# Residual x added by a transfer that adds on writing, in a streaming-encoder block

## The chip, the core and the metric

The kernel runs on one core of one Trainium2 chip. A core has TensorE for matrix products (PE in the profile; its weight loads, which run beside the products, are PEld), VectorE (DVE), ScalarE (ACT), GpSimd (POOL) and SyncE (SP), each with an instruction queue of its own that is worked off in order. Transfers between the chip's memory and the core's on-chip memory are issued from a queue (SP, ACT or POOL) and carried out by 16 DMA engines. The metric is the device time of one execution in microseconds (us).

## What is computed

One layer on x of 256 rows and 4096 columns, all in float32. After a norm, `xn @ w_in` gives the inputs of two branches, chunked attention and a convolution module, which yield y_a and y_c (2048 columns each). What matters here comes next:

```python
h = h + jnp.concatenate([y_a, y_c], axis=-1) @ w_out[i]      # residual: h is x here
gate = jax.nn.sigmoid(rms_norm(h, ple_norm_g[i]) @ w_ple_gate[i] + b_ple_gate[i])
h = h + gate * (p[i] @ w_ple[i])
return rms_norm(h, final_g)
```

So the output product (4096 by 4096) gets x added, the sum's rows need their sum of squares for the next norm, and the sum is the operand of the gate product (4096 by 4096).

## The kernel before

The 256 rows are two halves of 128 (index h), and columns go in blocks of 512. A product with a 4096-row weight is made by `mixed_product` for two column blocks (index j) at a time. It walks over 16 pairs of 128-row weight blocks in an order written out by hand (`dense`, `late`, `final`, ...). Every float32 operand is split in a high and a low part: `parts_of` lets ScalarE cast the weight block to the high part (wh, line 204) and VectorE subtract it to get the low part (wl, line 205), and TensorE makes three products of them. The pairs marked `*` are not made plainly (24 matmuls) but in seven combined products (21 matmuls), for which VectorE also adds weight blocks (ua, ub, lines 426 to 431). These seven go to four accumulators of the result, acc[h][j], and four helper accumulators P1, P5, P6 and P7. When the last seven-product pair is done, `on_helpers` combines the helpers into what has to be added to or subtracted from each quarter. In `helper_sums` (lines 464 to 471) that is one ScalarE copy and four VectorE additions.

Weight blocks come by transfers from SP's queue into five buffers, high and low parts have three buffers each. The order of instructions on each engine is the program's, except that a planner (of the tile framework) with a cost model of its own may bring instructions forward as their inputs and buffers allow. `later` is a queue of small pieces of work, and `fill` takes some from it after each pair.

The stage around the change is the loop over c0 = 0, 2, 4, 6 at lines 1045 to 1071: four output products, each for two column blocks. Before each, SP's queue loads the two blocks of x into the tiles `hc` (line 1049). `on_helpers` (lines 1054 to 1061) adds P1 to the first quarter of hc in place, builds the helpers' sums in scratch tiles z, and adds or subtracts those to the other three quarters. After the product, line 1070 adds the four accumulators to hc, and line 1071 queues four square sums (`square_sum`, line 500, ScalarE) for the norm. After the loop all that is left in `later` is done and `rstd_of` makes r_h, with a power on GpSimd.

Then come four gate products (`gated_pair` and a last one written out). Their operand is made from the tiles hc by `h_ahead`: TensorE transposes, ScalarE and VectorE split (lines 156 and 157) and combine them (lines 257 to 273). r_h is used first in the gate product's own `on_helpers` (line 1091).

Of the kernel before, what the change touches and what calls it, by code (L numbers as in the profile page):

```python
# [10 lines left out]
F32 = mybir.dt.float32  # L11
F32R = mybir.dt.float32r
AF = mybir.ActivationFunctionType
ALU = mybir.AluOpType
AX = mybir.AxisListType

P = 128
NB = 512
# [7 lines left out]
def hybrid_block(  # L26
# [23 lines left out]
    nc = tc.nc  # L50
    _, T, D = x.shape
    NH = T // P
# [15 lines left out]
    def pool(name, bufs, stack=ctx, side=0, **kw):  # L68
        return stack.enter_context(tc.tile_pool(name=name, bufs=bufs, side=sides[side], **kw))

    cpool = pool("cpool", 1)
    act = pool("act", 8)
# [107 lines left out]
    later = deque()  # L180

    def fill(n):
        for _ in range(min(n, len(later))):
            later.popleft()()
# [141 lines left out]

    def mixed_product(
        w, col, lhs, comb, order, on_helpers, ahead=None, fills=(0,), on_begin=None, apart=NB,
        left=(), begin=None,
    ):  # L330
# [64 lines left out]
        for n, (pair, seven) in enumerate(order):  # L395
# [59 lines left out]
            if n == last_seven:  # L455
                on_helpers(helper)
# [4 lines left out]
    tt, stt = nc.vector.tensor_tensor, nc.vector.scalar_tensor_tensor  # L461
    QUARTERS = ((0, 0), (1, 0), (0, 1), (1, 1))

    def helper_sums(helper, z):


        nc.scalar.copy(z[1][0], helper["P1"])
        tt(z[1][0], helper["P6"], z[1][0], ALU.add)
        tt(z[0][1], helper["P5"], z[1][0], ALU.add)
        tt(z[1][0], helper["P7"], z[1][0], ALU.add)  # L470
        tt(z[1][1], helper["P5"], z[1][0], ALU.add)

    def sum_tiles():

        t = [spool.tile([P, NH, NB], F32, tag="stage", name="z") for _ in range(2)]
        return t, [[t[j][:, h] for j in range(2)] for h in range(NH)]

    def scaled_pair(w, col, apart, order, r, fills, **kw):

        t, z = [], []  # L480

        def on_helpers(helper):
            for dst, src in zip((t, z), sum_tiles()):
                dst.extend(src)
            nc.scalar.activation(z[0][0], helper["P1"], AF.Identity, scale=r[:, :1])
            helper_sums(helper, z)
            for h, j in QUARTERS[1:]:
                nc.scalar.activation(z[h][j], z[h][j], AF.Identity, scale=r[:, h : h + 1])

        c = mixed_product(w, col, xT, xS, order, on_helpers, fills=fills, apart=apart, **kw)  # L490
        for h, j in QUARTERS:
            stt(
                z[h][j], c[h][j], r[:, h : h + 1], z[h][j],
                ALU.mult, ALU.subtract if j else ALU.add,
            )
        return t
# [443 lines left out]
    for c0, order in zip(range(0, CW // NB, 2), point):  # L940
        row = broadcast_row(b_pw, c0 * NB, 2 * NB, tag="stage")
        rows = [row[:, j * NB : (j + 1) * NB] for j in range(2)]
        ys, z = [], []
# [4 lines left out]
        def on_helpers(helper):  # L948
            y_tiles()
            z.extend([ys[j][:, h, :] for j in range(2)] for h in range(NH))  # L950
            tt(z[0][0], helper["P1"], rows[0], ALU.add)
            helper_sums(helper, z)
            for h, j in QUARTERS[1:]:
                tt(z[h][j], z[h][j], rows[j], ALU.subtract if j else ALU.add)

        acc = mixed_product(w_pw[0], c0 * NB, uS, uC, order, on_helpers)
# [35 lines left out]
    def before_last(make):  # L992

        return lambda pair: make(0) if pair == dense[-1][0] else None
# [29 lines left out]
    hs, hT, hS = [], [], []  # L1024
# [17 lines left out]
                embedding()  # L1042

    ssq_h = cpool.tile([P, NH, D // NB], F32, name="ssq_h")
    for c0 in range(0, D // NB, 2):
        for j in range(2):
            hc = act.tile([P, NH, NB], F32, tag="act", name="hc")
            c = c0 + j
            nc.sync.dma_start(
                hc, x[0, :, c * NB : (c + 1) * NB].rearrange("(h q) n -> q h n", q=P)  # L1050
            )
            hs.append(hc)

        def on_helpers(helper):
            _, z = sum_tiles()
            h00, h01, h10, h11 = (hs[c0 + j][:, h, :] for h in range(NH) for j in range(2))
            tt(h00, helper["P1"], h00, ALU.add)
            helper_sums(helper, z)
            tt(h01, h01, z[0][1], ALU.subtract)
            tt(h10, h10, z[1][0], ALU.add)  # L1060
            tt(h11, h11, z[1][1], ALU.subtract)

        acc = mixed_product(
            w_out[0], c0 * NB, yT, yS, dense if c0 else late, on_helpers,
            ahead=y_ahead if c0 == 0 else before_last(h_ahead) if c0 + 2 == D // NB else None,
            fills=(2,),
        )
        for h, j in QUARTERS:
            hc = hs[c0 + j][:, h, :]
            tt(hc, acc[h][j], hc, ALU.add)  # L1070
            later.append(partial(square_sum, ssq_h[:, h, c0 + j : c0 + j + 1], hc))
    fill(len(later))
    r_h = rstd_of(ssq_h, D, "r_h")

# [49 lines left out]
    c0 = n_f - 2  # L1124
    _, z = sum_tiles()
# [17 lines left out]
    def on_helpers(helper):  # L1143
# [4 lines left out]
    acc, add_left = mixed_product(  # L1148
        w_ple_gate[0], c0 * NB, hT, hS, final, on_helpers, fills=(4,), on_begin=on_begin,
        left=[None] * 3 + [kept] * 3,  # L1150
    )
# [119 lines left out]
```

## Time and profile before

| | us |
|---|---|
| three runs, median | 2039.71 |
| three runs, lowest and highest | 2039.58, 2039.95 |
| span of the profiled execution | 2038.9 |
| TensorE busy in it | 2021.0 |
| VectorE busy | 1905.7 |
| ScalarE busy | 1184.3 |
| GpSimd busy | 8.1 |

For the profiled execution the span from its first to its last instruction is what the profile gives; it lies 0.8 us under the median of the runs. A row of instructions in the profile reads: line, engine, operation, what it writes <- what it reads, how many, then durations and times. A row of a timeline reads: start in us, length in us, the instruction, and in brackets how long its engine stood idle before it and what ended that. In a row of waits, "A <- B: 0.2, 1, 0.2" means that A waited for B 0.2 us in total, once, the longest 0.2. "DMA to landing" is the time from a transfer's issue until its data is there. In a table of windows each row has the stretch, its length, and each engine's busy time with its instruction count, the granted clock of TensorE, the busy share of the DMA engines and what they moved.

### The profile page before, as it was taken

The page shows a single profiled execution, that of the slowest core. Times are in us where ns is not written, and L with a number is a line of the kernel's source. Part 1 is how long each engine was busy: PE and PEld are TensorE (multiplying, and loading weights), DVE is VectorE, ACT ScalarE, POOL GpSimd, SP SyncE. Part 2 cuts the span into 40 slices and gives each one's busy share as a digit, 9 for nine tenths or more (in the row PEclk, how much of TensorE's full clock was granted, in tenths as well). Part 3 has the DMA queues.
Part 4 walks back from the last instruction along what each step waited for, and adds up shares of the span by engine and source line. Part 5 has one row for each costly group of instructions (what it writes and reads, how often), then busy time and mean ns, then how long its engine had stood idle before and what let it go on. Part 6 is the DMA issues. An engine that isn't in the chain of part 4 may idle for free.

```text
span 2038.9 us, 26038 instructions
## 1 busy us (share of the span) xinstructions
PE 2021.0 (99%) x9106; PEld 1661.3 (81%) x9106; DVE 1905.7 (93%) x2720; ACT 1184.3 (58%) x1527; POOL 8.1 (0%) x19
## 2 busy tenths in 40 slices
PE   9999999999999999999999999999999999999997
PEld 7888888887888888888888888888888888888876
DVE  7999999899989998878899999999999999999998
ACT  7655535554555545576555656676565666655555
POOL 0000000000000000000000000000000000000000
PEclk9999999999999999999999999999999999999999
DMA  8566665666656665556666666676666656666765
GB/s 294 188 198 204 200 191 167 203 191 186 184 178 211 202 184 186 178 192 197 187 216 206 197 214 201 215 243 204 211 205 205 206 190 208 198 222 205 234 206 180
DMA packets 161853, 412.29 MB, mean 202 GB/s; under 512 B 12974, under 2 KB 16190, under 8 KB 161722
## 3 DMA queue, kind: packets, MB, share of 16 engines
q1 hardware_dynamic: 161072, 409.80, 62.9%
q8 instruction: 71, 1.16, 0.2%
q10 hardware_dynamic: 650, 0.84, 0.1%
q14 instruction: 60, 0.49, 0.1%
HBM read 406.39 MB, written 4.19 MB: 201 GB/s over the span
## 4 chain that ended last, share of the span: by engine, by line
PE 86%; DVE 10%; issue 2%; ACT 1%; DMA 0%; POOLq 0%; POOL 0%; ACTq 0%; DVEq 0%
PE acc L370 60%; PE acc_P L370 15%; PE acc L218 8%; DVE wl L205 4%; DVE cv L677 3%; PE tmp_ps L170 1%; DVE ul L205 1%; ACT wh L204 0%; PE tmp_ps L834 0%; PE tmp_ps L849 0%; DVE ub L431 0%; PE tmp_ps L867 0%; DVE ub L430 0%; DVE ua L426 0%; DVE ua L427 0%
## 5 line engine op out<-in xcount | busy, mean ns | idle before, releaser
L370 PE MATMUL acc<-wh,big_t 128*128 128x512 f32 x3788 | 1173.6, 391 | 0.9 <-DVE y_c L964 0.7
L204 ACT CAST wh<-wt 128x1024 fp32r<-128x1024 f32 (+1 forms) x737 | 714.7, 980 | 558.4 <-PE acc L370 335.4
L205 DVE TENSOR_TENSOR wl<-wt,wh 128x1024 fp32r<-128x1024 f32 (+1 forms) x737 | 823.7, 1130 | 48.2 <-ACT wh L204 43.0
L370 PEld LDWEIGHTS acc<-wh,big_t 128*128 128x128 f32 x3788 | 708.2, 188 | 147.9 <-DVE y_c L964 1.1
L370 PE MATMUL acc<-wl,big_t 128*128 128x512 f32 x1894 | 730.7, 391 | 0.2 <-DVE wl L205 0.2
L370 PEld LDWEIGHTS acc<-wl,big_t 128*128 128x128 f32 x1894 | 355.2, 188 | 75.7 <-DVE wl L205 2.0
L677 DVE SCALAR_TENSOR_TENSOR cv<-uT,dw,cv 128x255 f32<-128x255 f32 (+20 forms) x480 | 205.1, 463 | 1.3
L204 ACT CAST uh<-ub 128x1024 fp32r<-128x1024 f32 x122 | 128.3, 1052 | 123.9 <-DVE ub L431 99.9
L218 PE MATMUL acc<-wh,big_t 128*128 128x512 f32 x560 | 173.9, 392 | 0.0
L204 ACT CAST uh<-ua 128x1024 fp32r<-128x1024 f32 x122 | 128.6, 1054 | 72.5 <-DVE ua L427 65.3
L205 DVE TENSOR_TENSOR ul<-ub,uh 128x1024 fp32r<-128x1024 f32 x122 | 148.8, 1219 | 7.7 <-ACT uh L204 6.9
L370 PE MATMUL acc_P<-uh,big_t 128*128 128x512 f32 x504 | 154.4, 392 | 0.1
L205 DVE TENSOR_TENSOR ul<-ua,uh 128x1024 fp32r<-128x1024 f32 x122 | 148.6, 1218 | 0.6 <-ACT uh L204 0.4
L218 PEld LDWEIGHTS acc<-wh,big_t 128*128 128x128 f32 x560 | 105.5, 189 | 21.6
L370 PEld LDWEIGHTS acc_P<-uh,big_t 128*128 128x128 f32 x504 | 93.5, 188 | 22.3 <-ACT uh L204 3.6
L218 PE MATMUL acc<-wl,big_t 128*128 128x512 f32 x280 | 109.6, 392 | 0.0
L426 DVE TENSOR_TENSOR ua<-wt 128x512 f32<-128x512 f32 x122 | 83.7, 686 | 26.3 <-DMA wt<-in_w_in_dram 21.4
L370 PE MATMUL acc_P<-ul,big_t 128*128 128x512 f32 x252 | 96.5, 391 | 0.0
L427 DVE TENSOR_TENSOR ua<-wt 128x512 f32<-128x512 f32 x122 | 83.4, 684 | 4.6 <-DMA wt<-in_w_in_dram 3.5
L431 DVE TENSOR_TENSOR ub<-ub,wt 128x512 f32<-128x512 f32 x122 | 83.6, 685 | 1.0
L430 DVE TENSOR_TENSOR ub<-ua,wt 128x512 f32<-128x512 f32 x122 | 83.4, 683 | 0.3
L370 PE MATMUL acc<-uh,big_t 128*128 128x512 f32 x244 | 75.4, 390 | 0.0
(241 smaller groups left out, 1526.4 us busy)
## 6 DMA issues: line engine op xcount, KB each, us to landing
wt<-in_w_in_dram SPq DMA_DIRECT2D x447, 512.0 KB, 4.1
wt<-in_w_out_dram SPq DMA_DIRECT2D x128, 512.0 KB, 4.1
wt<-in_w_ple_gate_dram SPq DMA_DIRECT2D x128, 512.0 KB, 4.2
wt<-in_w_pw_dram SPq DMA_DIRECT2D x32, 512.0 KB, 4.6
hc<-in_x_dram SPq DMA_DIRECT2D x8, 512.0 KB, 5.6
wt<-in_w_ple_dram SPq DMA_DIRECT2D x8, 512.0 KB, 4.4
xin<-in_x_dram SPq DMA_DIRECT2D x7, 512.0 KB, 8.3
out_dram<-hc SPq DMA_DIRECT2D x12, 256.0 KB, 2.5
```

Of the source, the lines that this page charges most:

```text
L170: nc.tensor.transpose(pt[:, i * T + h * P : i * T + (h + 1) * P], src[:, h, b * P : (b + 1) * P], ident,)
L204: nc.scalar.copy(wh[:, :kc, :], wt[:, :kc, :]),
L205: nc.vector.tensor_tensor(wl[:, :kc, :], wt[:, :kc, :], wh[:, :kc, :].bitcast(F32), ALU.subtract),
L218: nc.tensor.matmul(acc, a, b[:, k, :], start=kb == 0 and kind == 0, stop=kb == kblocks - 1 and kind == 2,)
L370: nc.tensor.matmul(banks[name], a, b, start=name not in begun, stop=final and ends[name] == n and kind == 2 and not (left and name in "P2 ...
L426: plus(ua[:, 0], w0[:, 0], w0[:, 1])
L427: plus(ua[:, 1], w0[:, 1], w1[:, 1])
L430: plus(ub[:, 0], ua[:, 0], w1[:, 1])
L431: plus(ub[:, 1], ub[:, 0], w1[:, 0])
L677: nc.vector.scalar_tensor_tensor(cv[:, i, PAD - k :], uT[:, i, : T + k - PAD], dw[:, b, k : k + 1], cv[:, i, PAD - k :], ALU.mult, ALU.add,)
```

## The change

x is no longer loaded ahead of the product. The tiles hc now take the part that `sum_tiles` gave in the other products: P1 is copied into the first quarter by ScalarE, `helper_sums` builds the other quarters in hc itself, and after the product the accumulators are added (or, for the second block, the tile is subtracted from them). Then GpSimd's queue issues, for each of the two tiles, a transfer from x that adds to what lies in the tile. The square sums are queued behind that; they and all later readers of hc need the landed transfer.

```diff
     ssq_h = cpool.tile([P, NH, D // NB], F32, name="ssq_h")
+    def x_columns(c):
+        return x[0, :, c * NB : (c + 1) * NB].rearrange("(h q) n -> q h n", q=P)
+
     for c0 in range(0, D // NB, 2):
-        for j in range(2):
-            hc = act.tile([P, NH, NB], F32, tag="act", name="hc")
-            c = c0 + j
-            nc.sync.dma_start(
-                hc, x[0, :, c * NB : (c + 1) * NB].rearrange("(h q) n -> q h n", q=P)
-            )
-            hs.append(hc)
+        hs.extend(act.tile([P, NH, NB], F32, tag="act", name="hc") for _ in range(2))
+        z = [[hs[c0 + j][:, h, :] for j in range(2)] for h in range(NH)]
 
         def on_helpers(helper):
-            _, z = sum_tiles()
-            h00, h01, h10, h11 = (hs[c0 + j][:, h, :] for h in range(NH) for j in range(2))
-            tt(h00, helper["P1"], h00, ALU.add)
+            nc.scalar.copy(z[0][0], helper["P1"])
             helper_sums(helper, z)
-            tt(h01, h01, z[0][1], ALU.subtract)
-            tt(h10, h10, z[1][0], ALU.add)
-            tt(h11, h11, z[1][1], ALU.subtract)
...
         for h, j in QUARTERS:
-            hc = hs[c0 + j][:, h, :]
-            tt(hc, acc[h][j], hc, ALU.add)
-            later.append(partial(square_sum, ssq_h[:, h, c0 + j : c0 + j + 1], hc))
+            tt(z[h][j], acc[h][j], z[h][j], ALU.subtract if j else ALU.add)
+        for j in range(2):
+            nc.gpsimd.dma_start(hs[c0 + j], x_columns(c0 + j), accum_op=ALU.add)
+            later.extend(
+                partial(square_sum, ssq_h[:, h, c0 + j : c0 + j + 1], z[h][j]) for h in range(NH)
+            )
```

## The prediction

> **What bounds the kernel now.** I read the page first: busy times, then the chain that ended last.
>
> ```profile
> PE 2021.0 (99%) x9106; PEld 1661.3 (81%) x9106; DVE 1905.7 (93%) x2720; ACT 1184.3 (58%) x1527; POOL 8.1 (0%) x19
> ...
> PE 86%; DVE 10%; issue 2%; ACT 1%; DMA 0%; POOLq 0%; POOL 0%; ACTq 0%; DVEq 0%
> ```
>
> TensorE is busy 2021.0 of 2038.9 us, so over the whole span at most 17.9 us can come from feeding it better. Next, the stretches of the stage that changes: the four output products (first four rows; the last row is the first gate product), one row per product.
>
> ```profile
> core 0: us, PE busy (x) PEld busy (x) DVE busy (x) ACT busy (x) POOL busy (x), PEclk, DMA share, GB/s
> 1315.00:1417.45 102.45, 102.45 (x486) 85.27 (x484) 97.82 (x158) 66.81 (x98) 0.00 (x0) 1.00 0.69 223
> 1417.45:1499.00 81.55, 81.55 (x361) 67.56 (x360) 78.18 (x93) 48.85 (x59) 0.00 (x0) 1.00 0.63 207
> 1499.00:1581.00 82.00, 82.00 (x363) 67.89 (x363) 79.00 (x93) 49.28 (x60) 0.00 (x0) 1.00 0.63 208
> 1581.00:1664.00 83.00, 83.00 (x375) 68.64 (x374) 79.14 (x101) 51.20 (x65) 0.00 (x0) 1.00 0.62 204
> 1664.00:1746.00 82.00, 82.00 (x389) 68.27 (x388) 77.92 (x126) 54.90 (x86) 0.69 (x1) 1.00 0.62 199
> ```
>
> In every row PE's busy time equals the stretch, at a granted clock of 1.00. VectorE follows at 95 to 96%, the DMA engines work at 0.62 to 0.69, and GpSimd does nothing until 1664. From 1400 to 1710 us the waits of the weight loads have one row:
>
> ```profile
> PEld acc_P L370 <- DVE ul L205: 0.2, 1, 0.2
> ```
>
> So work taken from VectorE here can give TensorE 0.2 us, and a new delay costs its whole length once TensorE's cover is used up. The question is what can become late.
>
> **The parts that go, or change engine.** The tiles hc, over the whole span:
>
> ```profile
> L500 ACT ACTIVATE junk<-hc x33: 416/629/634, 1416.9 to 2028.5; 128x512 bf16<-128x512 f32 x31, 128x256 bf16<-128x256 f32 x2
> L500 ACT ACTIVATION_READ_ACCUMULATOR junk<-hc x33: 185/187/196, 1417.4 to 2028.8; 128x1 f32 x33
> L1070 DVE TENSOR_TENSOR hc<-acc,hc x16: 677/680/692, 1416.1 to 1667.9; 128x512 f32<-128x512 f32 x16
> ...
> L1049 SPq DMA_DIRECT2D hc<-in_x_dram x8: 368/379/386, 1321.6 to 1366.1; - x8
> ...
> L1057 DVE TENSOR_TENSOR hc<-acc_P,hc x4: 681/682/692, 1403.7 to 1648.9; 128x512 f32<-128x512 f32 x4
> L1059 DVE TENSOR_TENSOR hc<-hc,z x4: 679/680/681, 1409.7 to 1654.8; 128x512 f32<-128x512 f32 x4
> L1060 DVE TENSOR_TENSOR hc<-hc,z x4: 678/679/680, 1410.9 to 1656.0; 128x512 f32<-128x512 f32 x4
> L1061 DVE TENSOR_TENSOR hc<-hc,z x4: 681/682/683, 1411.5 to 1656.6; 128x512 f32<-128x512 f32 x4
> ```
>
> *VectorE:* lines 1057, 1059, 1060 and 1061 go: 16 instructions x 0.68 = 10.9 us, 2.7 per product. The 16 additions of line 1070 and the four helper sums stay, with other tiles. By the row above the gain for the end is 0.2 us at most; I take 0. It does leave room to catch up after a stall.
>
> *ScalarE:* four copies of P1 come in its place. The like copy, line 467:
>
> ```profile
> L467 ACT COPY z<-acc_P x4: 568/580/591, 1404.5 to 1649.6; 128x512 f32<-128x512 f32 x4
> ```
>
> 4 x 0.58 = 2.3 us on an engine that is 59 to 66% busy: 0. Without that cover it would be 2.3.
>
> *SyncE's queue:* eight issues go, with their waits: before, the queue also carried the next weight loads behind them.
>
> ```profile
> SPq L1049 <- PE tmp_ps L170: 14.9, 7, 6.6
> ```
>
> TensorE did not stop for these 14.9 us, so their end gives 0; the same 4 MB are moved later, two 512 KB transfers after each product.
>
> *The order of the rest* is redone by the planner, but on PE the same products stand in the same order around the four product ends. I take 0 for it.
>
> **What is new: ScalarE waits for the transfer.** Each of GpSimd's eight transfers waits for the additions into its tile. The 16 square sums of the stage (line 500) now wait for a transfer's landing instead of an addition, and ScalarE takes its instructions in order. In the built order of the changed program, after each of the first three products ScalarE has: all casts of the next product's pairs 1 and 0, two square sums (first transfer), one square sum (second transfer), and then the cast of pair 3's first weights. After the last product it has, behind the second landing: square sum, a transform's copy, square sum, and the cast for pair 3 of the first gate product. So the casts, VectorE's low parts behind them and then TensorE queue up behind the landing.
>
> How long may the landing take? First product end, with the additions of the next two, which come 81.4 and 163 us later at the same place of the order:
>
> ```profile
> 1416.15 2.47 DVE L1070 TENSOR_TENSOR hc<-acc,hc 128x512 f32<-128x512 f32 x4
> 1497.53 2.64 DVE L1070 TENSOR_TENSOR hc<-acc,hc 128x512 f32<-128x512 f32 x4
> 1579.13 2.64 DVE L1070 TENSOR_TENSOR hc<-acc,hc 128x512 f32<-128x512 f32 x4
> ...
> 1423.09 1.06 ACT L204 CAST wh<-wt 128x1024 fp32r<-128x1024 f32 x1 [1.66 <-PE acc L370]
> ...
> 1424.18 1.23 DVE L205 TENSOR_TENSOR wl<-wt,wh 128x1024 fp32r<-128x1024 f32 x1
> ...
> 1427.88 0.61 PE L370 MATMUL acc<-wh,big_t 128*128 128x512 f32 x2
> 1428.33 0.39 PE L370 MATMUL acc<-wl,big_t 128*128 128x512 f32 x1
> ```
>
> The last addition ends at 1416.15 + 2.47 = 1418.62. TensorE takes pair 3's high part at 1427.88 and its low part at 1428.33. Backwards from there: low part 1.23, cast 1.06, square sum 0.63 + 0.19 = 0.82. The second landing must be seen by 1428.33 - 3.11 = 1425.22, that is 6.6 us after the last addition. (The cast itself could not start before 1423.09 in any case, because its buffer was still being read: a landing within 3.6 us changes nothing at all.)
>
> Last product end:
>
> ```profile
> 1667.88 0.68 DVE L1070 TENSOR_TENSOR hc<-acc,hc 128x512 f32<-128x512 f32 x1
> ...
> 1671.22 1.04 ACT L204 CAST wh<-wt 128x1024 fp32r<-128x1024 f32 x1
> 1672.20 0.48 ACT L273 ACTIVATE comb<-tmp_ps,prm 128x256 f32<-128x256 f32 x1
> ...
> 1677.06 0.71 PE L370 MATMUL acc<-wh,big_t 128*128 128x512 f32 x2
> 1677.61 0.39 PE L370 MATMUL acc<-wl,big_t 128*128 128x512 f32 x1
> ```
>
> Behind the landing: 0.82 + 0.48 + 0.82 + 1.04 + 1.23 = 4.39, so it must be seen by 1677.61 - 4.39 = 1673.2. The last addition ended at 1668.56; with four instructions fewer ahead of it, it can end up to 2.7 earlier; I take half, 1667.2. That leaves 6.0 us.
>
> **How long it takes (L, from the last addition to ScalarE's release).** No row shows a transfer that adds or one issued by GpSimd. The nearest rows are the loads of the same 512 KB of x, line 1049 (all eight, then the two issued 0.9 us apart), and the stores at the end:
>
> ```profile
> DMA to landing us min/median/max: 3.7/5.6/7.5
> ...
> L1049 SPq DMA_DIRECT2D hc<-in_x_dram x2: 378/378/379, 1321.6 to 1322.5; - x2
> ...
> DMA to landing us min/median/max: 6.3/6.3/6.3
> ```
>
> ```profile
> DMA to landing us min/median/max: 2.0/2.5/3.1
> ```
>
> Two transfers again follow one another here (the first needs only the first two additions to end), beside the weights' stream, so I start from the pair, 6.3. The adding transfer must also fetch what lies in the tile: of 6.3, at most 6.3 - 2.0 (quickest store) = 4.3 is moving of data, and the additional fetch costs between nothing and as much again. I take half: L = 6.3 + 2.2 = 8.5, an estimate. Ends: 3.7 (quickest load, fetch and issue free) and 2 x 7.5 = 15.0 (slowest, doubled).
>
> [...]
>
> **The sum.** Three ends: 3 x (8.5 - 6.6) = 5.7 us. Last end: 8.5 - 6.0 = 2.5. Together 8.2 us on the profiled span of 2038.9: 2047.1. The median of the runs lies 0.8 above that span (2039.71), so 2047.9; 0.4% slower. Nothing is added for VectorE, which stands still during the stall: it has 2.7 us less per product to do. GpSimd's power for r_h comes behind the last transfers; its first reader comes over 60 us later:
>
> ```profile
> L1091 DVE SCALAR_TENSOR_TENSOR z<-acc_P,r_h,row x3: 742/745/751, 1740.1 to 1916.2; 128x512 f32<-128x512 f32 x3
> ```
>
> **Rivals.**
> *Hidden (not slower).* The landing comes within about 6.5 us of the last addition at all four ends. For it: weights of the same size and single x loads often land sooner (3.7 the quickest). Against it: two at a time, an added fetch, an issue in software. TensorE then does not stop: 2039.7, and the loss stays under 4.1 us as long as L is under 7.5 (4L - 25.8 = 4.1). It decides at that point. [...]
>
> *Much slower.* The adding transfer runs well below the load rate, or GpSimd's issue is held up, and the second waits for the first: L = 15 gives 3 x 8.4 + 9.0 = 34.2, 2073.9. For it: nothing seen bounds the adding rate. Against it: the DMA engines have 0.31 to 0.38 free. [...]
>
> *Faster.* VectorE's 10.9 us would have to reach TensorE, which waits 0.2 us for it in this stage: at best 2039.5. More than 4 us could only come from a luckier order later on.
>
> **Chances.** I count as no change what lies within 0.2%, 4.1 us, about what a measurement of this kernel can tell. ScalarE behind the landing with L between 7.5 and 12.6: 0.53, at 2044 to 2064 (4 x 12.6 - 25.8 = 24.6 more), the likeliest case's own range. Much slower, above 2064: 0.10. Hidden or within 0.2%: 0.33. Faster: 0.04. So faster 0.04, same 0.33, slower 0.63. The range must reach into the hidden case: 2039.4 to 2064.
>
> **What would show it.** ScalarE's square sums of hc waiting for a DMA from in_x_dram, four long waits of 2 to 8 us shortly after 1418, 1500, 1582 and 1667; right after each, PE or its weight loads waiting for the casts of pair 3 (line 204) or their low parts, about 2 us each; the eight GpSimd issues with their time to landing near 7 to 9; lines 1057 to 1061 gone and VectorE 11 us less busy; PE idle up by 8 and no clock change. I am wrong if these transfers land in under 6 us (no change), if ScalarE waits but TensorE does not, or if TensorE stops at another place, such as weights that land late (DMA share above 0.9 in those windows).

## The result, and the profile after

| | before | changed |
|---|---|---|
| median of four runs each, us | 2039.64 | 2075.93 |
| lowest and highest | 2039.18, 2039.95 | 2073.62, 2080.58 |
| span of the profiled execution | 2038.9 | 2071.8 |
| TensorE busy / idle in it | 2021.0 / 17.9 | 2031.0 / 40.8 |

The changed kernel is slower: ratio 1.0181, 95% interval 1.0169 to 1.0194. Its profiled execution is the quickest of its runs (2073.62), so its span stands 4.1 us under the median. The 32.9 us between the two spans are 22.9 more idle and 10.0 more busy time of TensorE, for the same 9106 matmuls.

The page of the changed kernel, busy times and the chain that ended last:

```profile
PE 2031.0 (98%) x9106; PEld 1663.5 (80%) x9106; DVE 1896.8 (92%) x2704; ACT 1187.2 (57%) x1531; POOL 18.1 (1%) x27
...
PE 82%; DVE 10%; DMA 3%; issue 3%; ACT 1%; ACTq 0%; POOLq 0%; POOL 0%; DVEq 0%
```

Its waits in the stage, 1300 to 1760 us:

```profile
ACT junk L500 <- DMA hc<-in_x_dram: 33.8, 8, 6.4
...
DVE ua L426 <- DMA wt<-in_w_out_dram: 21.0, 14, 3.9
PEld acc L370 <- ACT wh L204: 20.2, 4, 6.2
...
PE acc L370 <- ACT wh L204: 18.7, 4, 5.8
...
PE acc L370 <- DVE wl L205: 2.5, 2, 2.0
```

ScalarE's square sums wait eight times for the adding transfers, and four times TensorE then waits for ScalarE's cast, 18.7 us in all. At the first product end the timeline shows the whole sequence (last additions, the two issues, the square sums and the cast behind them, the matmul that waited):

```profile
1415.29 2.48 DVE L1062 TENSOR_TENSOR hc<-acc,hc 128x512 f32<-128x512 f32 x4
...
1416.88 1.37 POOL L1064 DMA_DIRECT2D hc<-in_x_dram  x1 [415.35 <-DVE hc L1062]
1423.09 1.24 POOL L1064 DMA_DIRECT2D hc<-in_x_dram  x1 [4.83 <-issue]
...
1422.91 0.63 ACT L500 ACTIVATE junk<-hc 128x512 bf16<-128x512 f32 x1 [2.92 <-DMA hc<-in_x_dram]
...
1430.61 0.63 ACT L500 ACTIVATE junk<-hc 128x512 bf16<-128x512 f32 x1 [6.22 <-DMA hc<-in_x_dram]
1431.15 0.19 ACT L500 ACTIVATION_READ_ACCUMULATOR junk<-hc 128x1 f32 x1
1431.24 1.03 ACT L204 CAST wh<-wt 128x1024 fp32r<-128x1024 f32 x1
...
1432.32 1.22 PE L370 MATMUL acc<-wh,big_t 128*128 128x512 f32 x2 [5.73 <-ACT wh L204]
```

The last addition ends at 1417.77 and ScalarE is released at 1430.61: L is 12.84 us. GpSimd issued the second transfer only 0.2 us after ScalarE had been released by the first, after 4.83 us in which it waited for nothing that the profile shows. The other three ends:

```profile
1506.82 2.48 DVE L1062 TENSOR_TENSOR hc<-acc,hc 128x512 f32<-128x512 f32 x4
...
1597.38 2.48 DVE L1062 TENSOR_TENSOR hc<-acc,hc 128x512 f32<-128x512 f32 x4
...
1693.04 1.28 DVE L1062 TENSOR_TENSOR hc<-acc,hc 128x512 f32<-128x512 f32 x2
...
1521.05 0.63 ACT L500 ACTIVATE junk<-hc 128x512 bf16<-128x512 f32 x1 [5.08 <-DMA hc<-in_x_dram]
...
1612.80 0.63 ACT L500 ACTIVATE junk<-hc 128x512 bf16<-128x512 f32 x1 [6.38 <-DMA hc<-in_x_dram]
...
1706.30 0.63 ACT L500 ACTIVATE junk<-hc 128x512 bf16<-128x512 f32 x1 [4.94 <-DMA hc<-in_x_dram]
```

So L is 11.75, 12.94 and 11.98 there. The stall brings a second loss, seen in short windows: two of the first end, then the stretches of lower clock at the first three ends, and one window of the last end (columns as in the prediction: after the engines the granted clock, the DMA share and GB/s):

```profile
1420.00:1426.00 6.00, 6.00 (x29) 4.95 (x28) 2.15 (x3) 1.45 (x4) 1.24 (x1) 1.00 1.04 315
1426.00:1432.00 6.00, 0.60 (x3) 0.17 (x1) 0.31 (x1) 1.39 (x3) 0.00 (x0) 0.98 0.52 100
1431.80:1438.63 6.83, 6.27 (x14) 4.48 (x15) 5.95 (x7) 3.89 (x7) 0.00 (x0) 0.50 0.50 148
1520.54:1527.37 6.83, 4.58 (x10) 3.18 (x11) 4.63 (x6) 4.79 (x8) 0.00 (x0) 0.50 0.31 85
1612.70:1619.53 6.83, 4.98 (x11) 3.48 (x12) 5.04 (x6) 4.79 (x8) 0.00 (x0) 0.50 0.34 98
1704.00:1716.00 12.00, 8.92 (x45) 6.97 (x44) 7.13 (x14) 7.95 (x16) 0.71 (x1) 1.00 0.56 173
```

TensorE does next to nothing from 1426 to 1432, and for 6.83 us from 1431.80 on the granted clock is 0.50. The same follows the stalls at the next two ends (4.63 and 5.75 us), but not the one at the last end (1.00, after 2.55 us). In these three stretches TensorE is busy for 6.27 + 4.58 + 4.98 = 15.8 us; at full clock the same matmuls would have taken about half of that (14 matmuls in 6.27 us in the third row, 29 in 6.00 in the first), so some 7.9 us are lost. The kernel before has one such stretch too (3.41 us from 497.98 on, 1.7 us lost), so the lower clock explains 6.2 of the 10.0 us by which TensorE's busy time grew; where the other 3.8 come from is not shown. Here the stalls of 4.63 us and more were followed by half clock and the one of 2.55 was not, but a shorter stall is not always safe, as e4_late shows below.

### The profile page after: what moved, and what is told of

Read it like the earlier page. It is cut to its first block, busy times and chain, and to the rows that moved or that the text cites. A ratio compares the mean times of both kernels' runs of the same rounds, so it can differ in the third digit from the quotient of the medians.

```text
span 2071.8 us, 26035 instructions
## 1 busy us (share of the span) xinstructions
PE 2031.0 (98%) x9106; PEld 1663.5 (80%) x9106; DVE 1896.8 (92%) x2704; ACT 1187.2 (57%) x1531; POOL 18.1 (1%) x27
## 4 chain that ended last, share of the span: by engine, by line
PE 82%; DVE 10%; DMA 3%; issue 3%; ACT 1%; ACTq 0%; POOLq 0%; POOL 0%; DVEq 0%
PE acc L370 58%; PE acc_P L370 14%; PE acc L218 7%; DVE wl L205 4%; DVE cv L677 3%; DMA hc<-in_x_dram 1%; DVE ul L205 1%; PE tmp_ps L170 1%; DMA wt<-in_w_out_dram 1%; DMA wt<-in_w_in_dram 1%; ACT wh L204 1%; DVE hc L1062 0%; PE tmp_ps L849 0%; DVE ua L427 0%; PE tmp_ps L834 0%
## 5 line engine op out<-in xcount | busy, mean ns | idle before, releaser
L370 PE MATMUL acc<-wh,big_t 128*128 128x512 f32 x3788 | 1179.3, 393 | 19.7 <-ACT wh L204 18.7
```

Of the source, the lines that this page charges most:

```text
L370: nc.tensor.matmul(banks[name], a, b, start=name not in begun, stop=final and ends[name] == n and kind == 2 and not (left and name in "P2 ...
```

## The experiments

All times are medians, and each ratio is against the kernel before in the same series (2039.8 us for the first four runs, 2041.4 for the next four, 2039.5 for the last four).

### Room for the issue (e1_room)

```diff
-    nc = _bacc.Bacc(..., dynamic_dma_scratch_size=1024)
+    nc = _bacc.Bacc(..., dynamic_dma_scratch_size=2048)
```

> The changed kernel with twice the room for the descriptors of transfers issued by GpSimd (2048 instead of 1024 bytes a partition); every engine's order is the same. Theory A, the second transfer of a pair waits at GpSimd until the first has landed because its descriptors find no room: now it is issued about 1.3 us after the first instead of 6.2, the pair lands 8 to 10 us after the last addition instead of 12.8, ScalarE waits 3 to 5 us less per end, 2048 to 2058 us. Rival B, adding transfers are let through one at a time, or the DMA engines are the limit: issues still 6 us apart, or issued early and landing as late as before, 2073 to 2081 us.

2071.52 us, ratio 1.0157 (1.0141 to 1.0172). GpSimd's and ScalarE's timeline, and the landings of the two transfers at the first end (DMA to landing, 1410 to 1430 us):

```profile
1416.09 2.62 POOL L1064 DMA_DIRECT2D hc<-in_x_dram  x2 [414.96 <-DVE hc L1062]
...
1429.92 0.63 ACT L500 ACTIVATE junk<-hc 128x512 bf16<-128x512 f32 x1 [6.48 <-DMA hc<-in_x_dram]
```

```profile
DMA to landing us min/median/max: 5.8/9.2/12.5
```

Rival B is what came, with a time 1.5 us below its range. The hold of 4.83 us hung on this setting: with 2048 both are issued back to back (2.62 us for the two, 0.3 us of hold at most at any end). That the setting is room for descriptors is the author's reading of it; the runs show the hold alone. But the second lands 12.5 us after its issue, where the first takes 5.8: it comes after the first whether or not the issue is held. ScalarE is released 12.96, 12.80, 12.45 and 9.96 us after the last addition at the four ends, so only the last end gains. That fits the DMA engines being the limit, because they are full from 1418 to 1428 us (share 1.03):

```profile
1418.00:1428.00 10.00, 7.84 (x35) 6.17 (x33) 3.66 (x5) 2.50 (x5) 0.71 (x1) 1.00 1.03 243
```

Hold or no hold makes at most about 5 us here, and the intervals of the two kernels overlap.

### Plain transfers (e2_plain) and none (e3_none)

```diff
-            nc.gpsimd.dma_start(hs[c0 + j], x_columns(c0 + j), accum_op=ALU.add)
+            nc.gpsimd.dma_start(hs[c0 + j], x_columns(c0 + j))
```

> The changed kernel with plain transfers in place of the adding ones, from the same queue, of the same size, at the same place of every order (x then overwrites the product, so this leaves the product out of h). If the addition itself is what takes the time (its fetch of the tile's contents takes room and engine time): both are issued at once, land in 4 to 5 us, and the time is 2040 to 2046 us. If any transfer issued by GpSimd waits for the one before it: still one after the other, about 4.5 us each, 2050 to 2060 us.

> The changed kernel without the eight adding transfers (x is left out of h). All theories: 2038 to 2041 us, as before, since TensorE never waited for VectorE in this stage. A time under 2036 would say that the 10.9 us taken from VectorE were worth something, one over 2044 that the new order of the instructions costs by itself.

Plain: 2055.21 us, 1.0076 (1.006 to 1.0091). None: 2040.93 us, 1.0005 (0.9996 to 1.0014). Without the transfers everything else of the change, VectorE's missing additions, ScalarE's copies, SyncE's shorter queue and the new order, comes to nothing that can be measured. The whole loss hangs on the transfers. VectorE, with less to do, stands longer for weights here than in the kernel before (3.3 us), and TensorE does not mind (1.2 us of waits in the stage, none for a low part wl). So this row is what later runs are to be compared with:

```profile
DVE ua L426 <- DMA wt<-in_w_out_dram: 15.2, 15, 1.7
```

The plain transfers are issued at once (1414.25 and 1415.43), and yet the time is in the second range. ScalarE is released 8.13, 8.13, 8.51 and 5.45 us after the last addition. That is about the L that was foretold for the adding ones (8.5), and with the prediction's deadlines it costs 1.5 + 1.5 + 1.9 + 0, some 5 us. The run lost 15, and TensorE's waits show a second cause beside the casts:

```profile
PE acc L370 <- DVE wl L205: 5.4, 6, 1.9
...
PE acc L370 <- ACT wh L204: 3.7, 4, 1.4
```

How the adding ones differ from plain ones is in the DMA queues. The changed kernel, 1415 to 1440 us (packets, MB, share of 16 engines):

```profile
q1 hardware_dynamic: 958, 3.51, 40.9%
q0 software_dynamic: 544, 1.05, 25.1%
```

With plain transfers, 1412 to 1440 us:

```profile
q1 hardware_dynamic: 1212, 4.44, 49.5%
q0 software_dynamic: 288, 1.05, 11.1%
```

The 1.05 MB added take 544 packets and 25.1% of 25 us, 6.3 us of all 16 engines; written plainly, 288 packets and 11.1% of 28 us, 3.1 us. Per MB that is 6.0 against 3.0, and weights take 2.9. So the adding transfers took twice the engine time of the plain ones. The eight landed in 5.7 to 7.5 us (median 6.1), the plain ones in 4.0 to 8.0 (median 4.6).

### Square sums later (e4_late)

```diff
+        later.extend([lambda: None] * (12 if c0 + 2 < D // NB else 20))
...
-                partial(square_sum, ssq_h[...], z[h][j]) for h in range(NH)
+                partial(square_behind, ssq_h[...], z[h][j]) for h in range(NH)
```

> The changed kernel with the square sums behind the adding transfers put six pairs later in ScalarE's order (ten pairs after the last product), held there; transfers as in the changed kernel, one after the other. Theory A, what costs is ScalarE's waiting in order ahead of the casts: 2039 to 2044 us, with no wait of ScalarE for hc and TensorE's clock back at 1.00. Rival C, the adding transfers crowd out the weights' loads on the DMA engines: VectorE still waits for weights and the time stays above 2055 us.

2051.11 us, 1.0053 (1.0037 to 1.007), between theory A and rival C, in the range of neither. `square_behind` keeps the place in ScalarE's order, so ScalarE no longer waits for x; r_h is made through the same queue, behind the last square sum. Some two thirds of the loss goes, and TensorE busy falls from 2031.0 to 2024.5 with it. The rest shows in these waits of the stage:

```profile
DVE ua L426 <- DMA wt<-in_w_out_dram: 26.3, 16, 4.2
...
PE acc L370 <- DVE wl L205: 5.8, 5, 1.8
```

Weights land late (5.0 us to landing in the median from 1412 to 1440 us, against 4.0 without transfers, where the same wait was 15.2 us, the longest 1.7, and TensorE had none for wl), VectorE stands, and TensorE waits for its low parts. After one of these short waits the clock was down too:

```profile
1607.20 0.50 PE L370 MATMUL acc<-wl,big_t 128*128 128x512 f32 x1 [1.85 <-DVE wl L205]
```

```profile
1608.00:1611.00 3.00, 3.00 (x8) 2.34 (x7) 3.00 (x4) 1.42 (x2) 0.00 (x0) 0.50 0.70 203
```

So a wait of 1.85 us was followed by half clock (0.50 over these 3.00 us; after one of 1.85 us in e6_one, pairs of matmuls took 1.06 us from 1437.88 to 1440.22, and 0.62 later), where the one of 2.55 us in the changed kernel was not (1.00 from 1704 to 1716). All ten waits of 3.3 us and more in this stage of the profiled runs were: three in the changed kernel (0.50), one in e7_first (0.79 over 8 us), and three each in e1_room and e10_w7, where the pair of matmuls behind each took 1.22 us. What decides for the shorter ones is not shown.

### Half the rows (e5_half), one tile of two (e6_one)

```diff
-            nc.gpsimd.dma_start(hs[c0 + j], x_columns(c0 + j), accum_op=ALU.add)
+            nc.gpsimd.dma_start(hs[c0 + j][:, :1], x_columns(c0 + j)[:, :1], accum_op=ALU.add)
```

> Both adding transfers of each product stay at their place and in their order, but each carries only the upper 128 rows (256 KB instead of 512); x is left out of the lower 128 rows. Theory A (the two transfers go one after the other at the rate of the adding transfer, and ScalarE's release comes with the second): in the changed kernel the second landed 12.8 us after the last addition for 1 MB; with a fixed part of about 2 us the half takes 2 + 10.8 / 2 = 7.4 us, about 0.8 us past the deadline of 6.6 at three ends and 1.4 at the last, 4 us of stall in all and no fall of the granted clock; with some 5 us for weights that still land late: 2044 to 2051. Theory B (a fixed cost for each adding transfer, whatever its size): the second still lands 11 to 13 us after the last addition and the time stays within 5 us of the changed kernel's, 2070 or more.

2053.77 us, 1.007 (1.0051 to 1.0089), 2.8 us above the range of theory A. The size of the landing follows A: 4.7 us in the median instead of 6.1, ScalarE released 6.7 us after the last addition (1424.08 against 1417.35; A's fixed part of 2 us was an assumption that no run shows for an adding transfer, and a line through 12.84 us and this leaves 0.6), and TensorE waits 0.2 us for a cast in the whole stage, instead of 18.7. The time did not follow, because the other wait grew: 6.9 us for low parts, instead of 2.5.

```diff
-            nc.gpsimd.dma_start(hs[c0 + j], x_columns(c0 + j), accum_op=ALU.add)
+            if j == 0:
+                nc.gpsimd.dma_start(hs[c0 + j], x_columns(c0 + j), accum_op=ALU.add)
```

> Only the first tile of each pair gets its x by an adding transfer; the second tile of each pair is left without x, so four transfers of 512 KB remain instead of eight. Theory A (the second transfer, behind the first, is what passes the deadline): the one transfer lands 6 to 7 us after the second addition, which is 1.3 us ahead of the last one, thus at or before the deadline of 6.6 us after the last addition; ScalarE's wait no longer reaches TensorE, and the time is 2040 to 2046, the last part for weights that land late behind the transfer. Theory B (any adding transfer at this place costs its share): half of the changed kernel's loss remains, near 2057.

2054.06 us, 1.007 (1.0052 to 1.0088). Theory A missed by 8 us or more, and B's 2057 is nearer. The transfer landed in 5.8 to 6.3 us, ScalarE was released 5.5 us after the last addition, inside the deadline, and TensorE had no wait for a cast. But again (waits of the stage):

```profile
DVE ua L426 <- DMA wt<-in_w_out_dram: 22.5, 15, 3.6
...
PE acc L370 <- DVE wl L205: 9.4, 7, 2.1
```

So below the deadline there is a second loss that the deadline knows nothing of.

### One product only (e7_first)

```diff
+        if c0:
+            for j in range(2):
+                nc.sync.dma_start(hs[c0 + j], x_columns(c0 + j))
...
+            if c0 == 0:
+                nc.gpsimd.dma_start(hs[c0 + j], x_columns(c0 + j), accum_op=ALU.add)
```

> The change is made for the first of the four output products alone; the other three load x ahead by SyncE and add it on VectorE as before. Theory A (each product end pays for itself: ScalarE's wait, the lower granted clock after TensorE's stop, late weights): a quarter to a third of the changed kernel's loss, 2047 to 2053, with one stop of TensorE of about 5 us for ScalarE's cast soon after 1420 and the granted clock below 0.9 in the 16 us behind it. Theory B (the stalls feed one another along the stage, or the loss is in later products): less than 4 us, below 2044.

2048.47 us, 1.004 (1.0026 to 1.0054): a quarter of the loss (0.0181 / 4 = 0.0045), as theory A has it. The planner put the cast of a sum behind the landing here, not that of a weight tile, and three loads of x on SyncE's queue were under way at the same time (8.4 us to landing in the median), so the stop is 3.33 us instead of 5:

```profile
1428.02 0.63 ACT L500 ACTIVATE junk<-hc 128x512 bf16<-128x512 f32 x1 [6.83 <-DMA hc<-in_x_dram]
...
1429.72 0.73 PE L370 MATMUL acc_P<-uh,big_t 128*128 128x512 f32 x2 [3.33 <-ACT uh L204]
```

```profile
1430.00:1438.00 8.00, 7.11 (x24) 5.08 (x24) 5.11 (x7) 5.03 (x11) 0.00 (x0) 0.79 0.63 135
```

The granted clock of 0.79 over 8 us comes to 3.4 us at half clock, if the rest ran at 1.00, after the stall of 3.33.

### Spread out (e8_spaced)

```diff
+        for h, j in QUARTERS:
+            later.extend([lambda: None, partial(add_x, hs[c0 + j], c0 + j, h)])
-            nc.gpsimd.dma_start(hs[c0 + j], x_columns(c0 + j), accum_op=ALU.add)
```

> All of the computation, with the adding transfers cut into four of 256 KB for each product, each held back until a cast of a later pair so that about one goes for each pair, and the square sums placed behind them. With the square sums alone placed later, 2051.1 was measured, and the rest of the loss lay in weights that landed late behind the transfers. Theory A (that rest is the burst of 1 MB at the product's end, crowding the weights that are due then): spread out, it falls to 2040 to 2045, and VectorE's and TensorE's waits for weights at the product's ends go back to below 1 us each. Theory B (adding transfers take the DMA engines' time from the weights wherever they are put): 2048 to 2054, with the waits spread over the product.

2051.36 us, 1.0058 (1.004 to 1.0077): theory B, no gain over the burst. But the first two of the four pieces were still issued back to back at three of the four ends (1414.91, both within 1.96 us), so half of the burst stayed, and theory A is tested only in part. VectorE's wait for weights is as long as with the burst:

```profile
DVE ua L429 <- DMA wt<-in_w_out_dram: 25.7, 19, 3.7
...
PE acc L373 <- DVE wl L207: 3.7, 6, 1.2
```

### More lead for the weights (e9_late_w7, e10_w7)

```diff
-                wt = wpool.tile([P, 2, NB], F32, tag="w", name="wt")
+                if wide and next(turn) % 7 > 4:
+                    wt = spool.tile([P, 2, NB], F32, tag="stage", name="wt")
+                else:
+                    wt = wpool.tile([P, 2, NB], F32, tag="w", name="wt")
```

> All of the computation; square sums placed later as before in the study (2051.1), and the weights of the four output products rotate through seven buffers instead of five (the two scratch tiles that the changed kernel leaves free in this stage), so that each load can be issued up to two tiles earlier. Theory A (what remains of the loss is weights that land late behind the adding transfers, with too little lead): the loads' longer lead covers it, 2039 to 2044, and TensorE's wait for low parts in the stage falls below 2 us. Theory B (the adding transfers take engine time that no lead gives back, or something else delays VectorE): 2048 to 2053.

2042.86 us, 1.002 (1.0011 to 1.003): theory A. The late square sums and seven weight buffers together bring the loss from 1.81% to 0.20%, with all eight adding transfers still there. Landings of the adding transfers in this run:

```profile
DMA to landing us min/median/max: 5.9/7.8/10.5
```

Waits of the stage:

```profile
DVE ua L433 <- DMA wt<-in_w_out_dram: 9.8, 7, 2.6
...
DVE ua L432 <- DMA wt<-in_w_out_dram: 5.2, 8, 1.2
...
PE acc L373 <- DVE wl L206: 0.7, 2, 0.4
```

Lines 432 and 433 are lines 426 and 427 of the changed kernel: 15.0 us together, against 27.9 in e4_late and 17.3 without transfers. Transfers did not get faster. The weights landed in 5.6 us in the median (1412 to 1440 us; 3.8 in the kernel before, 4.0 without transfers), and the longer lead covers that. What is left above e3_none, some 3 us by the two ratios, was not followed.

> All of the computation; the changed kernel with its square sums where they were, and seven weight buffers in the output products instead of five. Theory A (ScalarE's wait for the landing and late weights are two separate parts of the loss): the ScalarE part stays, 20 us or more with the clock's fall, and the part of the weights goes: 2060 to 2066. Theory B (the landing is late because the weights' stream is on the same DMA engines, and with more loads in flight it gets later still): 2072 or more.

2074.25 us, 1.017 (1.0155 to 1.0185), where ScalarE's square sums are as in the changed kernel. This is above A's range of 2060 to 2066 and is what B expected. B's reason is seen as well: L is 13.55, 13.14, 13.12 and 12.59, 13.1 in the mean instead of 12.4. Waits of the stage:

```profile
ACT junk L506 <- DMA hc<-in_x_dram: 36.7, 8, 7.0
...
PE acc L373 <- ACT wh L205: 20.2, 4, 6.4
...
DVE ua L432 <- DMA wt<-in_w_out_dram: 4.3, 6, 1.0
```

The two losses are not two parts of one sum. The lead does its part: VectorE waits 6.8 us for weights (4.3 and 2.5 for the next line) instead of 22.6 in the changed kernel. But there TensorE stood for ScalarE's cast (18.7 us) and hardly for low parts (2.5), so the lead buys nothing until ScalarE's wait is gone.

### Bytes or kind (e11_late_one, e12_late_plain)

Both have the late square sums; one has the second tile's transfer left out as in e6_one, the other transfers plainly as in e2_plain.

> Square sums placed later, and only the first tile of each pair gets its x by an adding transfer (x is left out of the second tile): four transfers of 512 KB instead of eight, without ScalarE's wait in the way. Theory A (the remaining loss goes with the bytes that the adding transfers move): about half of the 10 us that eight transfers left, 2043 to 2048. Theory B (the first transfer at the product's end does the damage, because the weights in flight at that moment are late for the next pair): 2049 to 2053. Theory C (what cost 12 us with one transfer and the square sums in place was ScalarE alone): 2039 to 2042.

> Square sums placed later, and the transfers write x in place of the product instead of adding (the product is lost). The instruction order is that of the kernel with late square sums and adding transfers (2051.1). Theory A (the adding transfers crowd out the weights because they take twice the engine time of a plain load): about half of the 10 us remains, 2043 to 2048. Theory B (any 1 MB on a second queue at this place delays the weights, whatever it costs the engines): 2049 to 2053.

One transfer: 2049.22 us, 1.0046 (1.0031 to 1.0061). Plain: 2053.63 us, 1.0067 (1.0052 to 1.0082). With two adding transfers it was 1.0053 (1.0037 to 1.007): the three can't be told apart. Half the bytes, or half the engine time, do not halve what the late weights cost, as far as the medians go: theory B in both (the plain run 0.6 us above its range), with a smaller saving left open by the intervals. VectorE's timeline with one transfer shows where it falls:

```profile
1426.19 0.69 DVE L426 TENSOR_TENSOR ua<-wt 128x512 f32<-128x512 f32 x1 [3.60 <-DMA wt<-in_w_out_dram]
```

And in the kernel without transfers:

```profile
1422.64 0.69 DVE L426 TENSOR_TENSOR ua<-wt 128x512 f32<-128x512 f32 x1 [0.97 <-DMA wt<-in_w_out_dram]
```

The first weights wanted after the product's end are waited for 2.6 us longer with one transfer, and 3.3 longer with two (the wait was 4.24 in e4_late). Why the second transfer adds so little was not separated.

## Why the prediction was wrong

It said slower, for the right reason, and gave a quarter of the price: 2047.9 us, with 2064 as the upper end, against 2075.93.

**What holds.** *The bound.* TensorE is it, and VectorE's freed time is worth 0: e3_none has VectorE 10.8 us less busy and stands at 1.0005. *The other zeros* (copies, SyncE's queue, the order): the same run bounds them together. (The rows have ScalarE 60 to 65% busy in the four products, not 59 to 66; nothing hangs on it.) *The mechanism.* ScalarE takes its square sums in order, and cast, low part and TensorE queue up behind the landing, at all four ends; e4_late removes this and takes 1.0181 to 1.0053. *The deadlines.* With the measured L, the prediction's own formula gives (12.84 - 6.6) + (11.75 - 6.6) + (12.94 - 6.6) + (11.98 - 6.0) = 23.7 us. TensorE waited 18.7 us for the four casts and 2.5 for low parts, 21.2 together, and its idle time grew by 22.9. So the deadlines are about right, in the sum some 2.5 us too strict. At the last end 2.0 us came by a way that the prediction does not list: the first landing held ScalarE's split of the gate product's operand, and VectorE's split and a low part behind it. Where L was made short (e5_half, 6.7 us), the wait for the cast went.

**The step that failed: the size of L.** It took 8.5 from the 6.3 us in which two loads of x, issued 0.9 us apart, both landed, plus half of the extra fetch. The runs put 12.4 in its place, the mean of the four ends. Two things in it were wrong, by about 2 us each. The two transfers of a pair do not land together like the loads: the second comes after the first, even when both are issued at once (e1_room: 5.8 and 12.5), and a plain pair already takes 8.1 to 8.5 at three of the ends instead of 6.3 (e2_plain). And the adding costs as much again as the writing, not half: 544 packets instead of 288, 6.0 us of the engines per MB instead of 3.0; it adds some 4 us to L, not 2.2. (That the tile is fetched for it is the author's explanation; no view shows the fetch itself.) This is 21.2 - 8.2 = 13.0 us of the error.

**The term that was missing: the clock.** "No clock change" was foretold. Stalls of 1.9 us might have left it alone, as the one of 2.55 at the last end did (two of 1.85 in other runs did not); those of 4.6 to 5.8 halved it. TensorE's busy time grew by 10.0 us, 6.2 of them by the clock. 8.2 + 13.0, 1.7 of other idle time and 10.0 make up the 32.9 between the spans.

**A term that was hidden: late weights.** They have no price in the sum, and in the changed kernel they cost little, because TensorE stands for the casts. But they would have made the sum too small at the foretold L as well: e2_plain, with an L of 8.1 to 8.5, lost 15 us, and e12_late_plain, where ScalarE waits for no x at all, 14.

**The rivals.** *Hidden* did not come: L was 11.75 us at the least. *Much slower* is what came, in mechanism (the second waits for the first) and in price: 34.2 foretold, without the clock and with an L too long at 15, two errors that cancel. It had 0.10 because the DMA engines had 0.31 to 0.38 free. That was a mean over 82 us; where the transfers ran the share was 1.04 (1420 to 1426; in e1_room 1.03 from 1418 to 1428). *Issue held up* was seen too, 4.8 to 5.1 us at each end, but e1_room shows that it decides little. *Weights that land late* stood among the signs of an error, with a DMA share above 0.9, and had no price. A longer lead for them gains nothing in the changed kernel itself (e10_w7), and some 0.3% as soon as ScalarE's wait is out of the way (1.0053 in e4_late, 1.002 in e9_late_w7).

No version by this route beats the kernel before: with the transfers taken out altogether, 2040.93 is reached.

## What to carry to other kernels

The transfer replaced additions on an engine with a few per cent of slack while another engine was the bound, and that bought nothing (VectorE 10.8 us less busy, 1.0005 in e3_none). What counted was the first instruction, in program order, that waits for its landing: look at what is queued behind that one. The two transfers of one queue came one after the other (5.8 and 12.5 us to landing in e1_room), and an adding one took twice the engine time of a plain one (6.0 and 3.0 us per MB): price them so until a run of the kernel at hand says otherwise, and read the free share of the DMA engines at the place of the burst (1.04), not over the stage (0.62 to 0.69). The three stalls of TensorE of 4.6 us and more cost about half as much again through the clock (7.9 us beside 16.1), and two of 1.85 us were followed by half clock as well; and a stall that was taken away uncovered another that hid beneath it (18.7 us of waits for casts gone in e5_half, 6.9 for low parts instead of 2.5).

## What the runs showed of the hardware

- An adding transfer of 512 KB from GpSimd landed in 5.7 to 7.5 us in the changed kernel and used about twice the packets and twice the engine time of a plain one (544 and 288 packets, 6.3 and 3.1 us of all 16 engines, for 1.05 MB). Its issue kept GpSimd for 1.2 to 1.4 us.
- With `dynamic_dma_scratch_size=1024` the second such issue was held 4.8 to 5.1 us in the changed kernel; with 2048 at most 0.3 us (e1_room).
- Weights loaded while these transfers ran landed in 5.6 us in the median instead of 3.8 (e9_late_w7 and the kernel before, 1412 to 1440 us).
- The granted clock was 0.50 for 6.83 us after the stalls of 4.63, 5.73 and 5.75 us in the changed kernel. After one of 3.33 us it was 0.79 over 8 us (e7_first), after one of 1.85 us 0.50 over 3.00 us (e4_late), and after another of 1.85 us pairs of matmuls took 1.06 us instead of 0.62 (e6_one). After one of 2.55 us it stayed at 1.00 (changed kernel, 1704 to 1716 us).
